# The first store of a masked softmax cut in two, the larger part held back for a mask

## The chip, the cores and the metric

The kernel runs on one core of a Trainium2 chip. The metric is device time in microseconds, from the launch of the program to its end, as the median of several runs. The profiler adds one execution of its own, from which the views quoted here come. It has a span, from the first to the last instruction, and a time of its own that lies a little above the span.

The core has five engines with a queue of instructions each: TensorE (PE), VectorE (DVE), ScalarE (ACT), GpSimd (POOL) and SyncE (SP). They meet only through semaphores: an instruction can wait for a count and can raise one. Transfers between the chip's main memory and the on-chip buffer are issued from an engine's queue and carried by 16 DMA engines, which all issuers share.

## The reference

The input is 16 batches of 8 x 256 rows with 256 columns each (float32, 2 MB a batch) and one length per batch, between 128 and 255. Each row becomes the softmax over its first `length` columns, and zero behind them:

```python
for b in range(batch):
    length = lengths[b]
    masked = x[b, :, :, :length].copy()
    masked = masked - np.max(masked, axis=-1, keepdims=True)
    exp_masked = np.exp(masked)
    result[b, :, :, :length] = exp_masked / np.sum(exp_masked, axis=-1, keepdims=True)
```

## The kernel before, in words

One batch is one tile: 128 partitions with 16 rows of 256 columns each, so 16 KB per partition, 2 MB in all. The buffer `xt` has eight slots of this size, and tile `b` lies in slot `b % 8`; everything is done in place. The names `half` (8 rows) and `quarter` (4 rows) cut a tile along the rows of each partition.

Each tile goes through five steps.

- Load. Tile 0 is loaded by SyncE in two halves (L136). Tiles 1 and 2 are loaded whole by GpSimd (L182). From tile 3 on GpSimd reads the tile's length and takes a load that brings only as many columns as are wanted (`pick`, L154; widths in steps of 8 or 16 columns); the columns that are left out are filled with zeros beforehand (L177). The program visits batches 1, 2, 3, 0, 4, 5 and so on. A load waits for the load two tiles before it, and from tile 8 on for the stores of the tile that had its slot.
- Mask. VectorE takes the minimum of the tile and a ramp that is very negative behind the length (L237). Each mask raises `s_min` by one. Tile 0's is done in halves, so `s_min` is 1 and 2 after them, 3 after the mask of tile 1 (the second tile).
- Exponential. ScalarE works through the 16 rows of each partition one by one and sums each row on the way (L344). Each half of a tile raises `s_exp`.
- Divide. VectorE takes the reciprocal of the sums of one half (L258) and multiplies the half by it (L261). Each half raises `s_out` by one.
- Store. SyncE issues the stores (L143), cut by `parts(b)`: tile 0 in two halves, tiles 1 to 7 as a half and two quarters, tiles 8 to 12 and 15 as halves, tiles 13 and 14 whole. A store waits at L140 until `s_out` has counted the half in which its last row lies. The first store of a tile from tile 2 on also waits at L142 until all the stores of the tile two before it have landed. Each tile's stores raise one of two semaphores, `s_st[b % 2]`, by 64 in all: 16 for each quarter.

All these are written out by hand in the order in which each queue runs them. VectorE's order at the beginning is: mask of tile 0 in two halves, divide of tile 0's first half, mask of tile 1, divide of tile 0's second half, mask of tile 2, both divides of tile 1, and from then on divide, mask of the next tile, divide. SyncE's order is the two loads of tile 0 and then the stores, tile after tile; a store that waits holds back all behind it.

At the end VectorE and TensorE look over the row sums (L293 to L304), and a slow path that subtracts the maximum is there for inputs that need it; with these inputs it does not run.

Of the kernel before, what the change touches and what calls it, by code (L numbers as in the profile page):

```python
# [21 lines left out]
def kernel(  # L22
# [6 lines left out]
    nc = tc.nc  # L29
# [5 lines left out]
    nt = rows // P  # L35
    half = nt // 2
    quarter = nt // 4
# [10 lines left out]
    def batch_of(pos):  # L48
        return pos + 1 if pos < ahead else 0 if pos == ahead else pos
# [7 lines left out]
    def parts(b):  # L57


        if b == 0:  # L60
            cuts = [0, half, nt]
        elif b < 8:
            cuts = [0, half, half + quarter, nt]
        elif b < 13 or b == batch - 1:
            cuts = [0, half, nt]
        else:
            cuts = [0, nt]
        return [slice(i, j) for i, j in zip(cuts, cuts[1:])]
# [30 lines left out]
    with tc.tile_critical(no_gpsimd_drain=True):  # L99
# [11 lines left out]
        s_min = sem("s_min")  # L111
# [22 lines left out]
        for h in range(2):  # L134
            s = slice(h * half, (h + 1) * half)
            nc.sync.dma_start(out=xt[:, 0, s], in_=x_f[batch_of(0), :, s]).then_inc(s_ld[h], 16)  # L136
        for b in range(batch):
            s_b = s_st[b % 2]
            for s in parts(b):
                nc.sync.wait_ge(s_out, 2 * b + (s.stop - 1) // half + 1)  # L140
                if b >= 2 and s.start == 0:
                    nc.sync.wait_ge(s_b, 64 * (b // 2 + 1))  # L142
                nc.sync.dma_start(  # L143
                    out=out_f[batch_of(b), :, s, :], in_=xt[:, b % slots, s, :]
                ).then_inc(s_b, 16 * ((s.stop - s.start) // quarter))
        nc.sync.wait_ge(s_st[0], 64 * (batch // 2 + 1))


# [259 lines left out]
```

## Time and profile before

| | us |
|---|---|
| median of three runs | 156.31 (156.23 to 156.35) |
| the profiled execution's own time | 156.43 |
| its span | 154.7 |
| VectorE busy | 116.9 (76% of the span) |
| ScalarE busy | 105.5 (68%) |
| GpSimd busy | 22.6 (15%) |
| moved by DMA | 61.57 MB, 398 GB/s over the span |

The views used below are these. The page's second part cuts the span into 40 equal slices and gives the busy share of each engine in tenths, and what the DMA engines moved. The timeline lists instructions by start and length in us, with the idle time before one and what ended it in brackets. The table of windows gives, for each stretch of time, its length, then for each of PE, PEld, DVE, ACT and POOL the busy time and the number of instructions, then TensorE's granted clock, the busy share of the DMA engines and GB/s. The list of queues gives packets, MB and the share of the 16 engines' time that the packets took: q0 carries what GpSimd issues, q1 what SyncE issues.

### The profile page before, as it was taken

The numbers are of one execution on the slowest core, as the hardware profiler recorded it, in microseconds if no ns is written. First come the engines' busy times: TensorE is split into PE (matmuls) and PEld (weight loads), VectorE is DVE, ScalarE is ACT, GpSimd is POOL, SyncE is SP. The second block draws the span as 40 slices with busy tenths as digits, with TensorE's granted clock in tenths as the row PEclk, the third lists the DMA queues.
The fourth block names the chain that finished last, engine by engine and source line by source line (L and its number), as shares of the span: only waits on it lengthen the run. The fifth ranks groups of instructions, "written<-read, shape, count | busy, mean of one in ns | idle before, by whom it ended". The sixth has DMA issues, their size and how long they took to land.

```text
span 154.7 us, 1304 instructions
## 1 busy us (share of the span) xinstructions
PE 0.3 (0%) x2; PEld 0.2 (0%) x2; DVE 116.9 (76%) x91; ACT 105.5 (68%) x514; POOL 22.6 (15%) x30
## 2 busy tenths in 40 slices
PE   0000000000000000000000000000000000000000
PEld 0000000000000000000000000000000000000000
DVE  1349769996969696979979696969697686968500
ACT  3096889749595959688695959595968829596000
POOL 4994000100220200202030020220010000000000
DMA  4999999999999999999999999999999999999992
GB/s 121 420 430 436 273 420 416 379 410 441 414 401 391 423 406 421 409 415 421 393 421 410 411 415 401 419 411 421 415 419 417 437 430 415 432 447 415 434 417 95
DMA packets 10357, 61.57 MB, mean 398 GB/s; under 512 B 866, under 2 KB 978, under 8 KB 6642
## 3 DMA queue, kind: packets, MB, share of 16 engines
q1 hardware_dynamic: 5616, 35.65, 56.0%
q0 software_dynamic: 4736, 25.89, 42.1%
q14 instruction: 3, 0.02, 0.1%
q10 hardware_dynamic: 2, 0.00, 0.0%
HBM read 27.98 MB, written 33.55 MB: 398 GB/s over the span
## 4 chain that ended last, share of the span: by engine, by line
DMA 43%; DVE 29%; ACT 10%; issue 7%; ACTq 3%; POOL 1%; POOLq 1%; SPq 0%; PE 0%
DMA xt<-in_x_dram 23%; DMA out_dram<-xt 19%; DVE xt L261 15%; DVE xt L237 12%; ACT xt L344 10%; ACTq L344 3%; DVE inv_sum L258 1%; POOL xt L177 1%; DMA word<-in_lengths_dram 1%; DVE ends L293 0%; ACTq L350 0%; POOLq L126 0%; SPq L143 0%; DVE bad L296 0%; DVE len_s L228 0%
## 5 line engine op out<-in xcount | busy, mean ns | idle before, releaser
L344 ACT ACTIVATE xt<-xt (+1 forms) x256 | 102.4, 402 | 34.4 <-DVE xt L237 34.4
L261 DVE TENSOR_TENSOR xt<-xt,inv_sum 128x2048 f32<-128x2048 f32 x32 | 73.4, 2292 | 1.1
L344 ACT ACTIVATION_READ_ACCUMULATOR xt<-xt (+1 forms) x256 | 47.9, 187 | 0.0
L237 DVE SCALAR_TENSOR_TENSOR xt<-down,len_s,xt 128x2048 f32<-128x2048 f32 (+1 forms) x17 | 37.8, 2221 | 9.0 <-DMA xt<-in_x_dram 9.0
L154 POOL DMA_DIRECT2D xt<-in_x_dram x13 | 13.8, 1065 | 89.5 <-DMA out_dram<-xt 50.7
L258 DVE RECIPROCAL inv_sum<-row_sum 128x8 f32<-128x8 f32 x32 | 6.4, 199 | 15.9 <-ACT xt L344 15.9
L177 POOL MEMSET xt<- 128x1536 f32 x5 | 6.7, 1400 | 1.1 <-DVE len_s L228 1.1
L337 ACT ACT_TABLE_LOAD x1 | 1.3, 1283 | 1.6 <-SPq L99 1.6
L220 DVE TENSOR_SCALAR down<-iota_i 128x256 f32<-128x256 int32 x1 | 0.3, 301 | 1.6 <-POOL iota_i L167 1.6
L182 POOL DMA_DIRECT2D xt<-in_x_dram x2 | 1.2, 606 | 0.0
L293 DVE TENSOR_REDUCE ends<-row_sum 128x1 f32<-128x256 f32 x2 | 0.7, 411 | 0.0
L207 PE MATMUL count<-bad,ones_c 128*1 128x3 bf16 x1 | 0.2, 165 | 142.5 <-DVE bad L296 142.5
L225 DVE CAST len_b<-word 1x16 bf16<-1x16 int32 x1 | 0.2, 165 | 0.4 <-DMA word<-in_lengths_dram 0.4
L228 DVE TENSOR_SCALAR len_s<-len_f 128x16 f32<-128x16 f32 x1 | 0.2, 175 | 0.4 <-PE len_f L205 0.4
L167 POOL IOTA iota_i<- 128x256 int32 x1 | 0.3, 332 | 0.6 <-SPq L99 0.6
L304 DVE TENSOR_REDUCE redo<-count 1x1 f32<-1x3 f32 x1 | 0.1, 149 | 0.3 <-PE count L207 0.3
L296 DVE TENSOR_SCALAR bad<-ends 128x1 bf16<-128x1 f32 x3 | 0.3, 149 | 0.0
L173 POOL MEMSET seed<- 1x1 f32 x2 | 0.2, 226 | 0.0
L207 PEld LDWEIGHTS count<-bad,ones_c 128*1 128x1 bf16 x1 | 0.1, 79 | 142.6 <-DVE bad L296 142.6
L337 ACT ACTIVATE warm<-const-float32-0.0 128x1 f32<-128x1 f32 x1 | 0.2, 203 | 0.0
L170 POOL MEMSET ones<- 1x128 bf16 x1 | 0.2, 195 | 0.0
L205 PE MATMUL len_f<-len_b,ones 1*128 1x16 bf16 x1 | 0.2, 168 | 2.6 <-DVE len_b L225 2.6
(8 smaller groups left out, 0.8 us busy)
## 6 DMA issues: line engine op xcount, KB each, us to landing
out_dram<-xt SPq DMA_DIRECT2D x21, 1024.0 KB
xt<-in_x_dram POOLq DMA_DIRECT2D x4, 2048.0 KB, 14.3
out_dram<-xt SPq DMA_DIRECT2D x14, 512.0 KB
xt<-in_x_dram POOLq DMA_DIRECT2D x3, 1728.0 KB, 16.3
out_dram<-xt SPq DMA_DIRECT2D x2, 2048.0 KB
xt<-in_x_dram POOLq DMA_DIRECT2D x2, 1600.0 KB, 19.1
xt<-in_x_dram POOLq DMA_DIRECT2D x2, 1280.0 KB, 14.0
xt<-in_x_dram SPq DMA_DIRECT2D x2, 1024.0 KB, 6.4
```

The costliest lines, as they stand in the source:

```text
L154: nc.gpsimd.dma_start(out=xt[:, slot, :, :w], in_=x_n[:, b, :, :w]).then_inc(s_sw[par], 16)
L167: nc.gpsimd.iota(iota_i, pattern=[[1, seq_k]], base=0, channel_multiplier=0).then_inc(s_iota, 1)
L177: nc.gpsimd.memset(xt[:, b, :, low:], 0.0).then_inc(s_fill, 1)
L182: nc.gpsimd.dma_start(out=xt[:, b], in_=x_f[batch_of(b)]).then_inc(s_ld[b + 1], 16)
L207: nc.tensor.matmul(count, lhsT=ones_c, rhs=bad, start=True, stop=True).then_inc(s_count, 1)
L220: nc.vector.tensor_scalar(out=down, in0=iota_i, scalar1=0.5, scalar2=-big, op0=ALU.add, op1=ALU.mult)
L237: return nc.vector.scalar_tensor_tensor(out=t, in0=down[:, None, lo:hi].to_broadcast([P, s.stop - s.start, hi - lo]), scalar=len_s[:, batc ...
L258: step(nc.vector.reciprocal(out=inv_sum[:, b, s], in_=row_sum[:, b, s]))
L261: nc.vector.tensor_tensor(out=t, in0=t, in1=inv_sum[:, b, s, None].to_broadcast([P, half, seq_k]), op=ALU.mult,).then_inc(s_out, 1)
L293: step(nc.vector.tensor_reduce(out=ends[:, k : k + 1], in_=values, op=op, axis=AX))
L337: nc.scalar.activation(out=warm, in_=nc.const_aps.tensor(0.0, (P, 1), F32), func=EXP)
L344: ins = nc.scalar.activation(out=e, in_=e, func=EXP, accum_out=sum_h[:, i, j])
```

## The change

The first store, of tile 0's first half (rows 0 to 7 of each partition, 1 MB), becomes two stores. Rows 0 and 1 (256 KB) are stored when that half has been divided, as the whole half was. Rows 2 to 7 (768 KB) wait, beside that, until `s_min` has reached 3, so until VectorE has masked the second tile. The count that the two raise on the tile's semaphore is 16 each, so that the tile's total remains 64.

```diff
         if b == 0:
-            cuts = [0, half, nt]
+            cuts = [0, 2, half, nt]
...
                 nc.sync.wait_ge(s_out, 2 * b + (s.stop - 1) // half + 1)
+                if b == 0 and s.start == 2:
+                    nc.sync.wait_ge(s_min, 3)
                 if b >= 2 and s.start == 0:
                     nc.sync.wait_ge(s_b, 64 * (b // 2 + 1))
                 nc.sync.dma_start(
                     out=out_f[batch_of(b), :, s, :], in_=xt[:, b % slots, s, :]
-                ).then_inc(s_b, 16 * ((s.stop - s.start) // quarter))
+                ).then_inc(s_b, 16 * max(1, (s.stop - s.start) // quarter))
```

All other instructions keep their order on every engine.

## The prediction

> **What bounds the kernel now.** I read the page's 40 slices first, then the end of the span, then the stretch around the first store.
>
> The slices of the page, below the headings "busy tenths" (DMA is the busy share of the 16 DMA engines, in tenths), and the queues under them (packets, MB, share of the engines' time):
>
> ```profile
> span 154.7 us, 1304 instructions
> ...
> DVE  1349769996969696979979696969697686968500
> ...
> DMA  4999999999999999999999999999999999999992
> GB/s 121 420 430 436 273 420 416 379 410 441 414 401 391 423 406 421 409 415 421 393 421 410 411 415 401 419 411 421 415 419 417 437 430 415 432 447 415 434 417 95
> ...
> q1 hardware_dynamic: 5616, 35.65, 56.0%
> q0 software_dynamic: 4736, 25.89, 42.1%
> ```
>
> The DMA engines are busy from the first loads to the last slice; VectorE (DVE) is not. Queue q0 carries the loads that GpSimd issues, q1 SyncE's stores (and its two loads at the start). One slice is conspicuous, the fifth (15.5 to 19.3 us): 273 GB/s though the engines are "busy".
>
> The end of the span, as the table of windows (engine columns, then granted clock, DMA share, GB/s) and VectorE's last large rows:
>
> ```profile
> 130.00:144.00 14.00, 0.00 (x0) 0.00 (x0) 12.02 (x9) 9.69 (x48) 0.00 (x0) 1.00 1.02 434
> 144.00:150.00 6.00, 0.17 (x1) 0.08 (x1) 1.29 (x8) 0.00 (x0) 0.00 (x0) 1.00 0.99 419
> 150.00:153.00 3.00, 0.00 (x0) 0.00 (x0) 0.00 (x0) 0.00 (x0) 0.00 (x0) 1.00 0.55 229
> ```
> ```profile
> 141.84 2.29 DVE L261 TENSOR_TENSOR xt<-xt,inv_sum 128x2048 f32<-128x2048 f32 x1
> 144.05 0.74 DVE L293 TENSOR_REDUCE ends<-row_sum 128x1 f32<-128x256 f32 x2
> ```
>
> VectorE's last divide ends at 144.13 us, and the DMA engines still move 6 us x 419 + 3 us x 229 GB/s = 3.2 MB of stores. So compute is not the end: the time is the bytes (the same before and after) over the rate. VectorE could be some microseconds later without moving the end, and being earlier buys nothing. What the change is worth is what it does to DMA time lost early on.
>
> Where is DMA time lost? First the timeline at the first store and the rest of VectorE's work there (start, length), then windows, then packets by queue:
>
> ```profile
> 13.48 0.42 SPq L143 DMA_DIRECT2D out_dram<-xt  x1
> ...
> 13.61 2.35 DVE L237 SCALAR_TENSOR_TENSOR xt<-down,len_s,xt 128x2048 f32<-128x2048 f32 x1 [0.15 <-DMA xt<-in_x_dram]
> ```
> ```profile
> 16.11 2.29 DVE L261 TENSOR_TENSOR xt<-xt,inv_sum 128x2048 f32<-128x2048 f32 x1
> 20.71 2.35 DVE L237 SCALAR_TENSOR_TENSOR xt<-down,len_s,xt 128x2048 f32<-128x2048 f32 x1 [2.31 <-DMA xt<-in_x_dram]
> ...
> 23.21 2.29 DVE L261 TENSOR_TENSOR xt<-xt,inv_sum 128x2048 f32<-128x2048 f32 x1
> ```
> ```profile
> 10.00:14.00 4.00, 0.00 (x0) 0.00 (x0) 3.49 (x4) 4.00 (x22) 2.35 (x2) 1.00 0.99 422
> 14.50:18.70 4.20, 0.00 (x0) 0.00 (x0) 3.87 (x3) 2.49 (x13) 1.16 (x1) 1.00 1.05 332
> 18.70:26.50 7.80, 0.00 (x0) 0.00 (x0) 5.72 (x5) 7.19 (x37) 0.00 (x0) 1.00 0.97 398
> 26.50:29.00 2.50, 0.00 (x0) 0.00 (x0) 2.47 (x3) 2.50 (x15) 0.00 (x0) 1.00 1.02 360
> 29.00:35.00 6.00, 0.00 (x0) 0.00 (x0) 5.96 (x4) 2.91 (x16) 0.56 (x1) 1.00 1.01 409
> ```
>
> ```profile
> 14.00:15.00 1.00, 0.00 (x0) 0.00 (x0) 1.00 (x1) 0.18 (x2) 0.45 (x1) 1.00 1.04 442
> 15.00:16.00 1.00, 0.00 (x0) 0.00 (x0) 1.00 (x2) 0.00 (x0) 0.72 (x1) 1.00 1.05 360
> ```
>
> Packets by queue in 10 to 12 us, 16 to 18 us and 26.5 to 29 us, one answer each:
>
> ```profile
> q0 software_dynamic: 50, 0.82, 95.5%
> ```
> ```profile
> q0 software_dynamic: 29, 0.48, 88.4%
> q1 hardware_dynamic: 5, 0.04, 4.8%
> ```
> ```profile
> q0 software_dynamic: 211, 0.87, 98.5%
> q1 hardware_dynamic: 16, 0.03, 3.4%
> ```
>
> A load packet of 16 KB takes 0.955 x 2 us x 16 / 50 = 0.61 us in 10 to 12 us, and 0.884 x 2 x 16 / 29 = 0.98 us in 16 to 18 us. The first store was issued at 13.48 us; by 16 to 18 us, 3 us later, q1 has moved five packets, yet the loads already run at 0.6 of their speed. The same again, milder: the third store follows the divide that ends at 25.50 us; in 26.5 to 29 us q1 moves almost nothing (it has run dry), and the rate falls to 360. So in both places where a store is issued to a dry q1, the loads slow from 1.0 to 1.5 us after the issue (442 GB/s up to 15 us, 360 after it) until the store's packets flow. The first episode loses 4.2 us x (1 - 332/422) = 0.90 us, the second 2.5 x (1 - 360/409) = 0.30 us. That the dry queue is the cause is a reading of two cases, not shown.
>
> **The change part by part.** *The split.* The store of 128 x 8192 bytes at 13.48 us becomes 128 x 2048 (256 KB) at the same time and 128 x 6144 (768 KB) later. Bytes and semaphore totals stay. Nobody soon needs them landed: the next SyncE store that asks for tile 0's total is tile 2's, and it cannot go before that tile's own divide, which follows two more divides and a mask. SyncE pays one more issue, 0.42 us by the row at 13.48; it waits anyway, for the divide that ends at 16.11 + 2.29 = 18.40 us. Were SyncE without that slack, 0.42 us would be the cost.
>
> *The added wait.* The third count of VectorE's mask comes when the mask that starts at 13.61 us ends, at 15.96 us. So the 768 KB are issued at 15.96 instead of 13.48, 2.5 us later. Behind them in SyncE's queue is the second half of tile 0, ready at 18.40: 15.96 + 0.42 = 16.4, so it is not delayed. The engines do not go idle for it, as GpSimd's issues of loads show (tiles 1 and 2, tile 3, tile 4):
>
> ```profile
> 4.37 1.21 POOL L182 DMA_DIRECT2D xt<-in_x_dram  x2
> 5.83 1.18 POOL L154 DMA_DIRECT2D xt<-in_x_dram  x1 [0.24 <-issue]
> ...
> 14.55 1.16 POOL L154 DMA_DIRECT2D xt<-in_x_dram  x1 [2.20 <-issue]
> ```
>
> q0 holds tiles 2, 3 and 4 then, and hardly a store packet flowed before 18 us in the kernel before either. Were q0 empty, 2.5 us of idle engines would be the cost.
>
> *The smaller packets.* A store packet's price, from the windows 29 to 32 us (8 KB packets) and 36 to 41 us (mostly 4 KB, and 17 four-byte ones):
>
> ```profile
> q1 hardware_dynamic: 96, 0.79, 64.0%
> q0 software_dynamic: 96, 0.46, 39.3%
> ```
> ```profile
> q0 software_dynamic: 113, 1.73, 80.7%
> q1 hardware_dynamic: 111, 0.41, 19.8%
> ```
>
> 8 KB: 0.64 x 3 x 16 / 96 = 0.32 us; 4 KB: 0.198 x 5 x 16 / 94 = 0.17 us. On a straight line 2 KB takes 0.09 and 6 KB 0.245, together 0.335 us instead of 0.32: with 8 packets on each engine, 0.12 us lost.
>
> *The share of the loads.* The first of these two answers shows 96 packets of each queue in 3 us: they take turns, one for one. A 2 KB store packet buys a load packet just as an 8 KB one did. A load packet beside it takes 0.393 x 3 x 16 / 96 = 0.20 us, so tile 0's stores take 8 x (0.09 + 0.20) + 8 x (0.245 + 0.20) + 8 x (0.32 + 0.20) = 10.0 us in place of 16 x 0.52 = 8.3 us. Before, they ended near 26.5 us; now near 28.2 us. The third store is issued at 25.50, or up to 2.31 us earlier (VectorE's wait for tile 2's load, if that load is not slowed), and so meets a q1 that is not dry. The second episode should go: -0.30 us. Bounds: 0 (it was not the dry queue) and -0.30.
>
> *The first episode.* It is what the change addresses. The store that comes to the dry queue is a quarter as large, 16 KB an engine rather than 64, for the 2.5 us until the rest is issued; by then tile 2's slowed load is nearly through. No row shows a small store into a dry queue. The nearest is the second episode, which cost 0.30 us beside smaller load packets. Ends: -0.90 us (the episode vanishes) and +0.50 us (it is prolonged by the 2.5 us to the second issue: 2.5 x (1 - 332/422) = 0.53). I take half of the episode, -0.45 us, an estimate: the store still comes to a dry queue, but with less. VectorE then gets tile 2 sooner; what is late next is ScalarE, but neither is the end.
>
> *Sum.* -0.45 - 0.30 + 0.12 = -0.63 us: the span 154.7 becomes 154.1, the profiled execution 156.43 becomes 155.80. The runs' median, 156.31, stands 0.12 us below that execution, so 155.7 us.
>
> **The rivals.** *It goes slower: the second part opens an episode of its own.* The slowing may hang on the issue, not on the dry queue: the issue at 15.96 us then keeps loads slow for the 4.2 us + 1 us that followed the one at 13.48, to about 21 us instead of 18.7. Price +0.53 + 0.12 = +0.65, or 156.95 us with the second episode left. It decides if the loads of 18.7 to 21 us stay under 360 GB/s. For it: the onset is timed by an issue, both times. Against: the store issued at 18.40 us met a busy q1, and 18.7 to 26.5 us ran at 398 GB/s.
>
> *Nothing moves.* The slowing belongs to the loads (tile 2's read towards its end, tile 3's towards its own), not to the stores. Only the packets' 0.12 us remain: 156.4 us. For it: both episodes also lie at the end of a load. Against: the load before ran at 422 to its end.
>
> *All of the first episode goes,* if 16 KB an engine is too little to disturb: -0.90 - 0.30 + 0.12 = -1.08, 155.2 us.
>
> *Each store pays a fixed cost on the full engines.* Then one more store would cost a start-up in series; the nearest row for a start-up is the 1.0 us from an issue to the slowing, so +1.1 us, 157.4 us. Against it: the slices from the tenth to the twentieth, with mostly 512 KB stores until about 70 us and 1 MB stores after, hold 391 to 441 GB/s throughout.
> The Trainium skill's page "DMA: Bandwidth & Descriptors", section "Rules for kernel authors", speaks against this change: for most bandwidth it asks for at least 1 MiB a DMA, and would have small transfers coalesced; the same page's fit has about 2 us fixed for each DMA, which in series would make 158.3 us. By the row of the slices the trace does not agree that smaller stores lower a full queue's rate.
>
> **How the numbers follow.** Half the first episode and all the second: 0.36, its own range 155.3 to 156.0. All of both: 0.14. Nothing moves: 0.16. An episode of the second part: 0.28. Fixed cost: 0.06. A difference of 0.2% (0.31 us) is about what a measurement can tell here. Faster by more: 0.36 + 0.14 = 0.50, less 0.01 for a forecast that falls short; within: 0.16 + 0.01; slower: 0.28 + 0.06 = 0.34. The range reaches from below all of both, 154.9, to just above the second part's episode, 157.1.
>
> **What would show it.** In the profile after: a row of 256 KB and one of 768 KB among the stores, the second issued near 16 us; the load packets of 15 to 18 us nearer 0.61 than 0.98 us; tile 2's mask starting between 19 and 20.4 us instead of 20.71; 26.5 to 29 us at 400 GB/s or more, with q1 flowing; the end of the DMA earlier by the same sum while VectorE's last divide may move more. The prediction is wrong if 14.5 to 18.7 us still shows about 332 GB/s, if the slow stretch only moves to 17 to 21 us, or if the gain there is given back in the mixed stretch after 29 us.

## The result and the profile after

The changed kernel takes 155.45 us (median of 6 runs, 155.16 to 155.77) against 156.27 us for the kernel before beside it: a ratio of 0.9948, 95% interval 0.9936 to 0.996, so 0.6 to 1.0 us faster. A second comparison gave 0.9958 (0.9943 to 0.9973). The profiled execution of the changed kernel has a span of 153.6 us and a time of 155.23 us; before they were 154.7 and 156.43.

The page's slices of the kernel after, and its queues:

```profile
span 153.6 us, 1306 instructions
...
DMA  4999999999999999999999999999999999999993
GB/s 107 422 439 435 311 385 424 421 403 434 427 400 389 424 409 419 409 420 411 398 428 404 413 412 404 416 416 415 411 427 421 421 426 433 420 444 435 425 418 154
...
q1 hardware_dynamic: 5760, 35.65, 56.4%
q0 software_dynamic: 4736, 25.89, 42.0%
```

The same bytes went through the same full engines. The fifth slice is up from 273 to 311 GB/s, but the sixth is down from 420 to 385, and the eighth is up from 379 to 421. The table of windows, for the stretches in which the prediction was made:

```profile
14.50:18.70 4.20, 0.00 (x0) 0.00 (x0) 4.00 (x3) 2.35 (x12) 1.16 (x1) 1.00 0.97 348
18.70:26.50 7.80, 0.00 (x0) 0.00 (x0) 6.86 (x5) 7.80 (x41) 0.00 (x0) 1.00 1.01 398
26.50:29.00 2.50, 0.00 (x0) 0.00 (x0) 2.47 (x3) 2.50 (x13) 0.00 (x0) 1.00 1.02 419
29.00:35.00 6.00, 0.00 (x0) 0.00 (x0) 4.90 (x4) 3.48 (x19) 0.56 (x1) 1.00 1.01 413
```

The second slow stretch is gone: 26.5 to 29 us runs at 419 GB/s instead of 360. The first stays: 348 instead of 332. The table counts a packet's bytes where the packet starts, so a short row is uneven where the size of the packets changes. To see the balance I therefore counted the bytes of all packets up to a given time, each packet spread evenly over its duration. The changed kernel is 0.42 us ahead (bytes at 415 GB/s) at 18 us, 0.04 us at 22 us, 0.45 us at 30 us and 0.51 us at 150 us. So what is won up to 18 us is lost again by 22 us: the first stretch is moved and hardly shortened. The second gives about 0.4 us, and nothing is given back in the 120 us that follow.

Packets by queue in the kernel after, 16 to 18 us and 26.5 to 29 us:

```profile
q0 software_dynamic: 38, 0.62, 96.5%
q1 hardware_dynamic: 6, 0.01, 1.6%
```
```profile
q1 hardware_dynamic: 95, 0.65, 62.0%
q0 software_dynamic: 104, 0.40, 40.2%
```

A 16 KB load packet takes 0.965 x 2 x 16 / 38 = 0.81 us in the first of them, between the 0.61 undisturbed and the 0.98 before. In the second, stores flow where before q1 was dry.

What was won is lost while the two rows of the first part go out, in packets of 2 KB (17.3 to 21.2 us). The packets by queue at 19 to 21 us after, then those of the kernel before at 20 to 22 us, when its 8 KB packets flow beside the same load of tile 3:

```profile
q0 software_dynamic: 103, 0.47, 71.6%
q1 hardware_dynamic: 107, 0.25, 31.4%
```
```profile
q1 hardware_dynamic: 67, 0.55, 64.7%
q0 software_dynamic: 64, 0.29, 35.1%
```

Together that is 359 GB/s after and 420 before. A load packet of 4.6 KB takes 0.716 x 2 x 16 / 103 = 0.22 us beside the 2 KB packets and 0.351 x 2 x 16 / 64 = 0.18 us beside the 8 KB ones.

SyncE's two issues and VectorE's third and fourth masks:

```profile
13.62 0.34 SPq L145 DMA_DIRECT2D out_dram<-xt  x1
```
```profile
16.20 0.34 SPq L145 DMA_DIRECT2D out_dram<-xt  x1
```
```profile
13.75 2.35 DVE L239 SCALAR_TENSOR_TENSOR xt<-down,len_s,xt 128x2048 f32<-128x2048 f32 x1 [0.16 <-DMA xt<-in_x_dram]
```
```profile
19.57 2.35 DVE L239 SCALAR_TENSOR_TENSOR xt<-down,len_s,xt 128x2048 f32<-128x2048 f32 x1 [1.03 <-DMA xt<-in_x_dram]
```

The 768 KB went at 16.20 us, and tile 2 was masked 1.1 us sooner than before. The end is still the drain of the stores.

### The profile page after: what moved, and what is told of

Its sections match the earlier page's. It is cut to its first block, busy times and chain, and to the rows that moved or that the text cites. A ratio compares the mean times of both kernels' runs of the same rounds, so it can differ in the third digit from the quotient of the medians.

```text
span 153.6 us, 1306 instructions
## 1 busy us (share of the span) xinstructions
PE 0.3 (0%) x2; PEld 0.2 (0%) x2; DVE 116.9 (76%) x91; ACT 105.3 (69%) x514; POOL 22.6 (15%) x30
## 4 chain that ended last, share of the span: by engine, by line
DMA 43%; DVE 29%; ACT 10%; issue 7%; ACTq 3%; POOL 1%; POOLq 1%; PE 0%; SPq 0%
DMA xt<-in_x_dram 32%; DVE xt L263 15%; DVE xt L239 12%; DMA out_dram<-xt 11%; ACT xt L346 10%; ACTq L346 3%; DVE inv_sum L260 1%; POOL xt L179 1%; DMA word<-in_lengths_dram 1%; DVE ends L295 0%; ACTq L352 0%; POOLq L126 0%; POOLq L161 0%; POOLq L156 0%; DVE bad L298 0%
```

## The experiments

**The two parts of the change alone.** The split without the wait (first diff), and the wait without the split (second):

```diff
-            cuts = [0, half, nt]
+            cuts = [0, 2, half, nt]
```
```diff
+                if b == 0 and s.start == 0:
+                    nc.sync.wait_ge(s_min, 3)
```

> The first store is cut into two rows and six rows, without the wait on the mask: both parts are issued from 13.5 us on. Dry-queue theory: the first episode costs what it cost before (the dry queue gets the full 64 KB an engine), the second episode goes because tile 0's stores run until about 28 us: -0.4 us against the kernel before, so half of the change's gain. Theory that only the wait matters (the loads of tile 2 are spared): no gain, 0 to +0.1 us. Theory that small packets alone spare the loads: -0.8 us, all of the gain.

> The first half is stored whole, but waits until the second tile's mask is done, at 16.0 us. Dry-queue theory: the first episode starts at 17 instead of 14.5 us and costs the same 0.9 us; tile 0's stores end later by what they started later, if they started later at all, and the second episode shrinks or goes: 0 to -0.4 us. Theory that the wait spares tile 2's load and that this is the gain: -0.8 us.

The split alone: ratio 0.997 (0.9958 to 0.9982). The wait alone: 0.9967 (0.9955 to 0.998). Windows of the split, then of the wait:

```profile
14.50:18.70 4.20, 0.00 (x0) 0.00 (x0) 3.92 (x3) 2.44 (x13) 1.16 (x1) 1.00 0.95 348
18.70:26.50 7.80, 0.00 (x0) 0.00 (x0) 7.01 (x5) 7.80 (x40) 0.00 (x0) 1.00 1.02 400
26.50:29.00 2.50, 0.00 (x0) 0.00 (x0) 2.46 (x3) 2.50 (x14) 0.00 (x0) 1.00 1.03 423
```
```profile
14.50:18.70 4.20, 0.00 (x0) 0.00 (x0) 3.97 (x3) 2.38 (x12) 1.16 (x1) 1.00 0.96 373
18.70:26.50 7.80, 0.00 (x0) 0.00 (x0) 7.21 (x6) 7.80 (x41) 0.00 (x0) 1.00 0.99 375
26.50:29.00 2.50, 0.00 (x0) 0.00 (x0) 2.47 (x3) 2.50 (x13) 0.06 (x1) 1.00 1.02 418
```

Either part alone does what the two do together: 26.5 to 29 us runs at 418 to 423 GB/s, and at 150 us they are 0.50 and 0.53 us ahead in bytes, as the changed kernel is. The wait alone runs 14.5 to 18.7 us faster, 373, and pays it back in 18.7 to 26.5 us, 375 instead of 398: it delays the first stretch. Its gain of 0.5 us (0.3 to 0.7) lies between what the two theories gave it. The split alone issues all of tile 0's first half from 13.53 us on, and it too runs 19 to 21 us at 345 GB/s, so the slow time there doesn't come from the second issue at 16.20 us; the 2 KB packets are common to both kernels. No run changes them alone. The split and the changed kernel once more, on one chip:

> The changed kernel once more, beside the split without the wait on one chip. The bytes moved by 150 us were 0.21 MB ahead of the kernel before in both, 0.5 us. Theory that the second episode is the whole gain: -0.4 to -0.6 us, the same as the split alone within its interval. Theory that the wait adds something of its own: -0.8 us, 0.2 to 0.3 us beyond the split.

> The split into two and six rows without the wait, for comparison with the changed kernel on the same chip: -0.5 us by the second-episode theory and by what was measured before.

They gave 0.9958 (0.9943 to 0.9973) and 0.9966 (0.9955 to 0.9978). The intervals largely overlap, so that the wait adds something to the split isn't shown.

**The second stretch alone.** The first store is as before; tile 0's second half goes as two quarters, which lengthens its stores by the turns of packets:

```diff
-            cuts = [0, half, nt]
+            cuts = [0, half, half + quarter, nt]
```

> The first store is as before; tile 0's second half goes as two quarters of 512 KB, with 4 KB packets and no wait. The first episode isn't touched. By the one-for-one turns of packets tile 0's stores end about 1.8 us later, near 28.3 us, so the third store finds a busy queue. Dry-queue theory: the second episode goes, -0.3 to -0.4 us, and 26.5 to 29 us runs at 400 GB/s or more. Theory that the slow stretch belongs to the end of tile 3's load: no change, 26.5 to 29 us at 360 GB/s still.

```profile
14.50:18.70 4.20, 0.00 (x0) 0.00 (x0) 3.94 (x3) 2.41 (x13) 1.16 (x1) 1.00 1.00 326
...
26.50:29.00 2.50, 0.00 (x0) 0.00 (x0) 2.47 (x3) 2.50 (x14) 0.00 (x0) 1.00 1.03 410
```

The ratio is 0.9989 (0.998 to 0.9999). The first stretch is as it was, the second is filled, and the kernel is ahead by 0.37 us in bytes at 150 us; the time shows 0.17 us of it (0.02 to 0.31), less than the 0.3 to 0.4 us expected. That the stretch goes when q1 doesn't run dry is shown; how a dry q1 makes it is the next question.

**A dry queue made on purpose.** The changed kernel, in which tile 1's first store waits until tile 3 is masked:

```diff
+                if b == 1 and s.start == 0:
+                    nc.sync.wait_ge(s_min, 5)
```

> The changed kernel, but tile 1's first store waits until the fourth tile is masked, near 31.4 us, instead of going at 24.4 us. Tile 0's stores end near 28 us, so the store queue is dry for some 3 us and the store then comes to it while only loads run, at no load's end. Dry-queue theory: a new episode from about 32.5 us with 300 to 380 GB/s for 2 to 4 us, +0.3 to +1.0 us against the changed kernel, so the gain over the kernel before is gone. Theory that slow stretches belong to a load's end: no such stretch, and the time of the changed kernel within 0.1 us.

The ratio is 1.0004 (0.9992 to 1.0016): the whole gain is lost again. But the profile contradicts the theory's picture. SyncE's issue, then the windows around it, then the packets by queue at 29 to 31 us and at 33 to 34.5 us (q1 has none in either):

```profile
31.43 1.80 SPq L147 DMA_DIRECT2D out_dram<-xt  x4
```
```profile
28.00:30.00 2.00, 0.00 (x0) 0.00 (x0) 2.00 (x2) 1.27 (x7) 0.35 (x1) 1.00 1.02 366
30.00:31.50 1.50, 0.00 (x0) 0.00 (x0) 1.47 (x3) 0.00 (x0) 0.21 (x1) 1.00 1.03 346
31.50:33.00 1.50, 0.00 (x0) 0.00 (x0) 1.50 (x1) 1.40 (x7) 0.00 (x0) 1.00 1.16 434
33.00:34.50 1.50, 0.00 (x0) 0.00 (x0) 0.79 (x1) 1.50 (x9) 0.00 (x0) 1.00 0.95 404
```
```profile
q0 software_dynamic: 142, 0.68, 101.7%
```
```profile
q0 software_dynamic: 37, 0.61, 94.9%
```

The slow time starts at 28 us, long before the store is issued at 31.43, and it is over by about 32.5 us, although the store's packets begin only at 35.1 us. What changes there is the load. Up to 31.9 us tile 4's load runs alone, 200 of 256 columns, in packets of 4.8 KB: 1.017 x 2 x 16 / 142 = 0.23 us each, where such a packet took 0.20 us in turns with stores. From 32.0 to 32.7 us, engine by engine, tile 5's load takes over, whole rows in packets of 16 KB: 0.949 x 1.5 x 16 / 37 = 0.62 us, nearly full speed, and q1 is as dry as before. (The 434 in the row from 31.5 us is the count at the start of the first large packets; spread evenly it is 363.) So the reading is now that a dry q1 costs time only while a load of narrow rows is alone on the engines.

**That claim, tested by the width.** One kernel holds the whole first half until tile 2 has landed, so that narrow loads are alone for some 5 us. A second does the same and loads tile 3 in all columns. Their edits to the kernel before, the first and then what the second adds:

```diff
+                if b == 0 and s.start == 0:
+                    nc.sync.wait_ge(s_ld[3], 16)
```
```diff
-        pick(v_len, 0, ahead, 1, [160, 176, 192, 208, 224, seq_k])
+        pick(v_len, 0, ahead, 1, [seq_k])
```

> The first half is stored whole once tile 2's load has landed, so no store shares the engines with that load. Dry-queue theory: the episode comes all the same, about 1 us after the issue at 19.2 us, now at the cost of tile 3's load; the third store finds a busy queue, so only the second episode goes: -0.3 to -0.5 us. Theory that the first episode belongs to the load of tile 2 with its 16 KB packets: the first episode goes as well, -0.8 to -1.2 us.

> The kernel that holds the whole first half until tile 2 has landed, with tile 3 loaded in all 256 columns instead of 192: 0.52 MB more, 1.25 us at 418 GB/s. There the loads of tile 3 ran alone in packets of 4.6 KB at 326 to 331 GB/s from 19 to 23 us. Theory that a load of narrow rows cannot fill the engines alone: the stretch from 18 to 22 us runs at 420 GB/s or more, the 1 us lost there is won, and the time is 0 to +0.5 us against the kernel it is made from, in spite of the bytes. Theory that the wait for a store's start slows any load: still 330 GB/s, and +1.2 us.

The held kernel: 0.9984 (0.9974 to 0.9995). With the wide tile 3: 1.0021 (1.0012 to 1.003). Windows of the first, then of the second; the store is issued at 19.59 and 19.23 us and flows from 23.7 and 23.5 us:

```profile
14.50:17.00 2.50, 0.00 (x0) 0.00 (x0) 2.46 (x3) 1.09 (x7) 1.16 (x1) 1.00 1.02 439
17.00:19.00 2.00, 0.00 (x0) 0.00 (x0) 1.65 (x1) 2.00 (x11) 0.00 (x0) 1.00 0.91 346
19.00:21.00 2.00, 0.00 (x0) 0.00 (x0) 1.47 (x1) 2.00 (x11) 0.00 (x0) 1.00 1.04 329
21.00:23.00 2.00, 0.00 (x0) 0.00 (x0) 1.97 (x3) 2.00 (x11) 0.00 (x0) 1.00 1.04 329
```
```profile
17.00:19.00 2.00, 0.00 (x0) 0.00 (x0) 1.45 (x1) 2.00 (x12) 0.00 (x0) 1.00 1.04 438
19.00:21.00 2.00, 0.00 (x0) 0.00 (x0) 1.84 (x1) 2.00 (x12) 0.00 (x0) 1.00 1.00 410
21.00:23.00 2.00, 0.00 (x0) 0.00 (x0) 1.97 (x3) 2.00 (x12) 0.00 (x0) 1.00 0.96 270
```

In the first kernel the last whole rows of tile 2 are still on their way until 18.9 us. In 19 to 21 us only tile 3's width differs: 329 GB/s narrow, 410 wide (328 and 424 with the packets spread evenly), with no store moving in either. That is the second stretch's cause, shown: narrow rows alone. Narrow rows also come in smaller packets, 4.6 KB against 16, and which of the two matters the runs don't separate. In time the wide load was 0.6 us slower than the narrow one, for bytes worth 1.25 us at the usual rate; 0 to 0.5 us was expected. The Trainium skill's page "DMA: Bandwidth & Descriptors", section "Specifications", names 512 B as the least size for full rate; here rows of 768 B, alone, stay at 329, and the measurement decides. The row of 21 to 23 us shows something else: 2 us after a store's issue the wide load falls too, to 270 (292 spread evenly). In the narrow kernel the issue changes nothing, 329 before and after it. So the first stretch has a cause of its own, and it came only with a store pending (issued, with no packet moved yet): without one, 14.5 to 17 us ran at 439.

**What the first stretch is.** Three attempts. A small store ahead of the first one, of 128 KB of the ramp to rows that are stored again later, sees whether only the program's first store pays:

```diff
+        nc.sync.wait_ge(s_min, 2)
+        nc.sync.dma_start(out=out_f[batch_of(0), :, half, :], in_=down).then_inc(s_warm, 16)
...
+                if b == 0 and s.start == half:
+                    nc.sync.wait_ge(s_warm, 16)
```

> The kernel before with one store more: at 10.6 us, while only tile 1's load runs, 128 KB of the ramp go to rows of tile 0's second half, which that half's own store overwrites after it has waited for this one. Dry-queue theory, the loss going with the bytes that the queue takes in at first: the small store costs up to 128 KB of loads, 0.3 us, at 11.6 to 14 us, and the first real store has its episode of 0.9 us as before if the queue is dry again by then: 0 to +0.6 us. Theory of a cold start that only the first store of the program pays: the slow stretch moves to 11.6 to 15 us and 14.5 to 18.7 us runs near 420 GB/s, at 0 to +0.3 us in all.

```profile
12.00:14.50 2.50, 0.00 (x0) 0.00 (x0) 2.35 (x2) 2.27 (x12) 0.34 (x1) 1.00 1.01 429
14.50:18.70 4.20, 0.00 (x0) 0.00 (x0) 3.96 (x3) 2.39 (x12) 1.16 (x1) 1.00 1.02 333
```

Ratio 1.0011 (0.9999 to 1.0023), and the stretch stands where it stood: it is no start-up of the store queue. Nor does it need a dry q1: the small store's packets ran from 14.26 to 20.0 us. And while that store itself was pending, from 10.72 us on, the loads kept their speed, 429 GB/s. Next, GpSimd's issue of tile 4's load, which falls into the stretch, is moved behind tile 2's mask, in the kernel before and in the changed one:

```diff
+        nc.gpsimd.wait_ge(s_min, 4)
         with nc.Fori(0, batch // 2 - 2, 1, engines=[POOL]) as q:
```

> The kernel before, with GpSimd's issue of tile 4's load (14.55 us) held until tile 2 is masked, near 23 us. Tile 3's load keeps the engines busy until about 28 us, so nothing is missed. Theory that the first slow stretch (15 to 18.6 us) comes from the descriptors that GpSimd writes meanwhile beside the store's start: the stretch goes, -0.8 to -1.0 us. Theory that it belongs to the store's start beside the loads of tiles 2 and 3: the stretch stays and the time is within 0.3 us of the kernel before.

> The same delay of tile 4's load in the changed kernel. If GpSimd's descriptors are the cause of the first stretch, both gains add up: -1.5 us against the kernel before. If not, the time of the changed kernel, -0.6 to -0.8 us.

The issue then falls at 25.45 and 25.31 us. They gave 1.0012 (0.9994 to 1.003) and 0.9952 (0.9939 to 0.9965), the times of the kernel before and of the changed one, so no time. In the kernel before the stretch stayed, at 314 GB/s. In the changed one's profile 14.5 to 18.7 us ran at 419, but there GpSimd's first loads had started 0.5 us later and lost 0.8 us at 8 to 12 us; by 20 us its bytes were level with the kernel before. Last, the late issue together with a wide tile 3, so that no narrow load stands behind tile 2:

> The kernel before with tile 4's load held until near 23 us, as in the last experiment, and tile 3 loaded in all 256 columns (0.52 MB more, 1.25 us). Now no narrow load stands behind tile 2's wide one when the first store is issued at 13.5 us. Theory that the first slow stretch comes from a narrow load queued behind, with a store pending: 14.5 to 18.7 us runs at 400 GB/s or more instead of 314, the 0.9 us is won, and the time is +0.2 to +0.5 us against the kernel before. Theory that a store pending beside any load is enough: 310 to 340 GB/s in that stretch, and +1.1 to +1.4 us.

Windows of it, twice, and of the late issue with narrow tile 3:

```profile
14.50:18.70 4.20, 0.00 (x0) 0.00 (x0) 3.94 (x3) 2.42 (x13) 0.00 (x0) 1.00 0.98 355
18.70:26.50 7.80, 0.00 (x0) 0.00 (x0) 6.87 (x5) 7.80 (x40) 1.18 (x1) 1.00 1.00 422
```
```profile
16.00:18.00 2.00, 0.00 (x0) 0.00 (x0) 1.97 (x3) 1.72 (x9) 0.00 (x0) 1.00 0.86 283
18.00:20.00 2.00, 0.00 (x0) 0.00 (x0) 0.91 (x2) 2.00 (x11) 0.00 (x0) 1.00 1.07 430
```
```profile
14.50:18.70 4.20, 0.00 (x0) 0.00 (x0) 3.85 (x3) 2.50 (x13) 0.00 (x0) 1.00 1.03 314
```

Neither theory has it: the stretch is shorter and shallower, 355 instead of 314, and over by 18 us, but with a store pending a wide load still falls to 283 for 2 us (329 spread evenly). The ratio is 0.9995 (0.9983 to 1.0007): 0.52 MB more were loaded at no cost in time, where 0.2 us or more was expected. Part of the first stretch thus seems to go with the narrow rows behind tile 2, by one profile of each kernel. What a pending store does to a load that is alone stays open, and so does why it did nothing to tile 5's load at 33 us in the kernel with the dry queue, or to the loads at 12 to 14.5 us beside the small store.

## Why the prediction was right, and where it was not

The forecast, 155.7 us within 154.9 to 157.1, faster, held; measured is 155.45. Step by step:

- *The bound is DMA time, and compute is not the end.* Right. In the changed kernel and with either part alone the lead in bytes at 30 us stayed to 150 us within 0.1 us.
- *The added wait holds nothing up.* Right: the second part was issued at 16.20 us (15.96 forecast), and the engines stayed busy.
- *The share of the loads.* Right, and by it the gain comes about. Packets of the two queues take turns whatever their size (107 of 2 KB beside 103 load packets, 67 of 8 KB beside 64), so small store packets stretch tile 0's stores over the time when q1 had been dry. The split and the quarters reach this by smaller packets, the wait by a later start.
- *The second episode, -0.30 us.* Near in size, about 0.4 us by the bytes between 26 and 30 us, and right that a dry q1 matters. Its reason was wrong. The prediction put it on a store issued to a dry q1; the runs show it is the narrow load left alone, and in the kernel with the dry queue it was slow for 3 us before any issue.
- *The first episode, -0.45 us.* This step failed. It was to cost half because a quarter of the bytes came first. Up to 18 us it did: the lead in bytes grew from -0.05 us at 14 us to 0.42 us. But 18.7 us was too early an end for the window: the slow time ran on to 21 us, which the prediction itself had named as a sign of being wrong, and by 22 us the lead was 0.04 us. The slower rival had foreseen this time, but not its reason: the split alone is slow there without a second issue.
- *The smaller packets, +0.12 us.* Too small by these traces. The store packets took what was forecast (0.084 us for 2 KB, 0.234 us for 6 KB). What the term put at nothing is that a load packet beside them takes 0.22 us, not the 0.20 us reckoned or the 0.18 us beside the 8 KB packets of tile 0 before. With 420 GB/s as the measure, 19 to 21 us at 359 costs 2 x (1 - 359/420) = 0.29 us, an estimate. Together this term and the first episode came to a gain of 0.09 us, where -0.45 + 0.12 had promised 0.33; no run separates the two.
- *The sum, -0.63 us.* The bytes explain 0.51 us of it by 150 us. The runs show 0.82 us (0.6 to 1.0) and 0.66 us (0.42 to 0.89, from the second ratio). The rest lies in the last 4 us, in which the engines finish one after another: the last data packet ends at 153.0 us before and 152.0 us after, while the bytes were only 0.5 us ahead. In the second profile of the changed kernel it ends at 152.3 us, with a lead of 0.61 us at 150 us, so most of that tail's gain belongs to one execution. What sets the tail wasn't tested. That the sum came so near is in part luck: two of its three terms brought 0.09 us in place of 0.33, the third brought 0.1 us more than forecast, and the tail, which was in no term, the rest.

The rival by which nothing moves had the slow stretches belong to the loads. It was wrong on the outcome, but nearer than the main theory on the second stretch: the loads' own rows make it, and stores in between hide it. The rival by which all of the first episode goes fails with that episode, though its 155.2 us was no farther from the result than the forecast. A fixed cost of 1.1 us for one more store is excluded: the split alone has one more and gained 0.5 us.

## What to carry to other kernels

When the DMA engines are full from end to end, a change is worth what it does to the stretches in which they are busy but slow; find these by bytes per window, not by busy share. Loads that fetch part of each row may need stores beside them to fill the engines, so keep the store queue from running dry while they run; a smaller packet in the queue that should last longer does that, within limits: here the 2 KB packets beside narrow rows moved 359 GB/s in all, 8 KB ones 420. Before putting a slow stretch on the event it follows, make the stretch without the event.

## What the runs showed of the hardware that was not expected

- Loads of 768 to 800 B rows alone run at 329 to 346 GB/s, whole rows at 404 to 439 outside the slow time after a store's issue. The narrow ones beside stores in 8 KB packets move 416 to 420 in total, beside 2 KB packets 345 to 359.
- From a store's issue to its first packet passed 3.4 to 4.3 us when loads filled the engines (issue 13.48, first packet 16.92 us in the kernel before; 16.16 and 20.41 in the one with the wait alone).
- Fetching 0.52 MB that nobody needs, to make one load's rows whole, cost no time in the kernel with the late issue (0.9995), and 0.6 us, half of its bytes' time, in the one that holds the first store.
